# Plain float32 products on two 64-column halves of TensorE in place of split rounded operands, in a two-layer hybrid backbone

## The chip, the cores and the metric

The kernel runs on one core of one Trainium2 chip. The metric is device time in microseconds of one execution. The profile is of one execution, taken by the hardware profiler; the page and the trace rows come from it. Engines are named as the profile names them: PE is TensorE (its weight loads are listed apart, as PEld), DVE is VectorE, ACT is ScalarE, POOL is GpSimd, SP is SyncE, which issues most DMAs here.

## What is computed

1024 latent tokens and 256 context tokens of width 1024 go through two layers and a last RMSNorm. Both layers are `x += gate * mixer(adaLN(RMSNorm(x)))`. Layer 0 is windowed attention with 16 query heads of 64 columns, 4 key heads and a sink logit per head; layer 1 is multi-head latent attention of every latent token over all 1280 tokens. The core of it, cut from the reference:

```
# layer 0: q, k, v, g = split(h @ w_in);  q, k of latent tokens get axial rope
s_loc = einsum("bqhgd,bkhd->bhgqk", q, k) * scale          # own block of 128 and its two neighbours
s_ctx = einsum("bqhgd,bchd->bhgqc", q, kc) * scale         # all 256 context tokens
p = softmax_with_sink(concatenate([s_loc, s_ctx]), sink)
yx = (p @ v * silu(gx)) @ w_out
# layer 1: cq, ckv, kr, g = split(h @ w_in)
q = rms_norm(cq, q_norm) @ w_uq                            # 16 heads of 64 + 32 (rope)
kv = rms_norm(ckv, kv_norm) @ w_ukv                        # 16 heads of 64 + 64
s = (qn . kn + qr . kr) * scale                            # kr is shared by the heads
yx = (softmax(s) @ v * silu(gx)) @ w_out
```

All inputs and outputs are float32.

## The kernel before

**Split operands.** Before, most products are made of three terms. An operand x is kept as two rounded float32 arrays (type `F32R`): `hi`, a rounded copy made by ACT, and `lo`, the rest, `x - hi`, made by DVE or POOL (`split`, L279 to L282). `mm3` (L284 to L288) then issues three matmuls into the same PSUM bank, hi by hi, lo by hi, hi by lo: lines L286, L287 and L288 of the profile. All split operands live in one large SBUF arena `R` of type `F32R` (arena_r), plain float32 data in a second, `F` (arena_f). PSUM is the tile `PB` of eight banks of 512 columns.

**Stages.**

1. The opening: adaLN columns (L840, L850), norm and transposes (L883), and layer 0's values (`v_part`, L912 and L917, which are the same three terms).
2. Layer 0's projections in blocks of 256 columns (`proj_t`), each 128 x 512 piece eight steps of `mm3`, while DVE works through the adaLN vectors of both layers (L508) that are summed over partitions on PE (L519: float32 matmuls with one column of ones, each into its own group of 32 columns of the array).
3. Layer 0's attention, 40 units of one tile of 128 queries and one key head with its four query heads (`UnitA`). `score` makes a head's logits: K stands as hi and lo in the upper and lower 64 rows, so that two matmuls (L698, L699) of 128 rows give a piece, 256 context keys and 256 or 384 window keys. DVE masks and takes the minimum (L705), ACT the exponential (L711), PE turns blocks of 128 keys (L728), the result is split, and `PV` applies it in two terms (L738) to V, whose hi and lo stand side by side in the 128 columns. `outproj` is `mm3` again.
4. Layer 1's projections, among them two rounds of sums that save products (`set_steps`), and the expansion of K and V per head from `ckvT` (`make_K`, `make_V`).
5. Layer 1's attention, 16 units of a pair of heads and 512 queries (`UnitB`). For each block of 128 keys `score` issues five terms, each for the two heads at once in the upper and the lower 64 rows of the array (L1820); ACT makes the exponential (L1830); POOL sums the exponentials of the ten blocks (L1836, DVE in the last unit). `top` (L1786) makes rounded logits of the next unit for its maxima, reduced on DVE (L1792), turned (L1800) and put into q as four extra rows. `PV` (L1843) is plain float32: two heads, each a matmul of 128 rows and 64 columns, in the left and the right half of the array. `fin2` (L1854) sums the denominators over partitions, float32 in two halves too. POOL and DVE prepare the layer's output weights between units (`wo_cut`), part of which takes a trip through DRAM (`wb_d`).
6. The output product in sums that save products (`out_sets`), norm and stores.

**What sets the order.** The opening and stages 2 and 5 are issued in the order of the code. From the last blocks of stage 2 up to the start of stage 5 the instructions are recorded in a `Plan` and issued by a list scheduler (`emit`): each engine takes, of what is ready by the planner's costs, the oldest. The cost of a matmul in it is

```
if eng == "tensor":
    half = 0.5 if aps[1].shape[0] < 128 else 1
    return (0.108 if name == "transpose" else half * (0.0135 + n * 0.000417)), 0.45
```

with n the columns of the result, whatever the type. Engines run their own queues in order; semaphores are set between them.

Of the kernel before, what the change touches and what calls it, by code (L numbers as in the profile page):

```python
# [28 lines left out]
R_KB = 152  # L29
# [188 lines left out]
def kernel(ctx: ExitStack, tc: tile.TileContext, t, out, dbg=None):  # L218
# [7 lines left out]
    R = cpool.tile([128, R_KB * KB], F32R, name="arena_r")  # L226
# [6 lines left out]
    q0_d = dpool.tile([4, 2, 2, 64, NT, 2, 128], F32, name="q0_d")  # L233
    g0_d = dpool.tile([8, 128, TOK], F32, name="g0_d")
    x1_d = dpool.tile([TOK, D], F32, name="x1_d")
    qn_d = dpool.tile([8, 128, 2, SEQ], F32, name="qn_d")
    qr_d = dpool.tile([4, 128, 2, SEQ], F32, name="qr_d")
# [3 lines left out]
    wb_d = dpool.tile([18, 128, 2, 512], F32, name="wb_d")  # L241
# [37 lines left out]
    def split(hi, lo, src, lo_eng=None):  # L279

        nc.scalar.copy(hi, src)  # L281
        (lo_eng or nc.vector).tensor_sub(lo, src, hi.bitcast(F32))  # L282

    def mm3(o, a, b, first, last):  # L284
        (ah, al), (bh, bl) = a, b
        nc.tensor.matmul(o, ah, bh, start=first, stop=False)  # L286
        nc.tensor.matmul(o, al, bh, start=False, stop=False)  # L287
        nc.tensor.matmul(o, ah, bl, start=False, stop=last)  # L288
# [46 lines left out]
    def norm_x(src, xr, junk):  # L335
        x = xr.next()
        load(out=x, in_=src)
        st = sm_ring()
        nc.scalar.activation(junk, x, AF.Square, accum_out=st[:, 0:1])
        nc.gpsimd.tensor_scalar(st[:, 1:2], st[:, 0:1], 1.0 / D, EPS, ALU.mult, ALU.add)  # L340
        nc.gpsimd.tensor_tensor(st[:, 2:3], st[:, 1:2], mhalf, ALU.pow)
        nc.vector.tensor_scalar_mul(x, x, st[:, 2:3])
        return x

    def turn_x(x, xt, j):
        for q in range(2):
            ps = shp(pst(), 4, 128)
            for c in range(4):
                nc.tensor.transpose(ps[:, c, :], x[:, (4 * q + c) * 128 : (4 * q + c + 1) * 128], ident)
            nc.scalar.copy(xt[:, 4 * q : 4 * q + 4, j * 128 : j * 128 + 128], ps)  # L350

    def build_x(p, src, xr, xtr, junk):

        xt = shp(xtr.next(), 8, 256)
        for j in range(2):
            turn_x(norm_x(src(2 * p + j), xr, junk), xt, j)
        return xt

    def build_h(p, xt, hT, A, B, fast=False, ks=range(8)):

        w = 1 if p == 0 else 0
        for k in ks:
            nc.vector.tensor_scalar(xt[:, k, :], xt[:, k, :], A[:, k, w : w + 1], B[:, k, w : w + 1], ALU.mult, ALU.add)
            if k % 2:
                hi = hT[:, 0, k - 1 : k + 1, :]
                nc.scalar.copy(hi, xt[:, k - 1 : k + 1, :])
                eng = nc.vector if fast or k % 4 == 1 else nc.gpsimd
                eng.tensor_sub(hT[:, 1, k - 1 : k + 1, :], xt[:, k - 1 : k + 1, :], hi.bitcast(F32))

# [13 lines left out]

    def load_w(dst, src, stage, nk, n, lo_eng=None, col0=0, k0=0):

        per = max(1, 512 // n)
        for k in range(k0, nk, per):
            st = shp(stage.next(), per, n)
            load(out=st, in_=src[k * 128 : (k + per) * 128, col0 : col0 + n].rearrange("(k p) n -> p k n", p=128))
            split(dst[:, 0, k : k + per, :], dst[:, 1, k : k + per, :], st, lo_eng or nc.gpsimd)  # L390
# [17 lines left out]
    hT = [r_at(16 * p, 2, 8, 256) for p in range(NP)]  # L408
    wst = [80, 96]
    kT = r_at(112, 4, TOK)  # L410
    V = r_at(132, NT, 4, 128)
    cosa = f_at(0, SEQ)
    sina = f_at(10, SEQ)
    stg = Ring(F, [4, 6, 8], 512)
    ev = Ring(F, [38, 40, 42, 44, 46], 512)
    qst = Ring(F, [34, 48], 1024)
# [24 lines left out]
    def fetch(bi, eng=nc.gpsimd):  # L441

        wt[bi] = r_at(wst[bi % 2], 2, 8, 256)
        src = w_in[:, blocks[bi] : blocks[bi] + 256].rearrange("(k p) n -> p k n", p=128)
        got = []

        def get(i):
            got.append(shp(stg.next(), 2, 256))
            load(out=got[i], in_=src[:, 2 * i : 2 * i + 2, :])

        def cut(i):
            ks = slice(2 * i, 2 * i + 2)
            split(wt[bi][:, 0, ks, :], wt[bi][:, 1, ks, :], got[i], eng)

        def second():
            cut(0)
            get(3)
            cut(1)
            cut(2)

        for i in range(3):
            get(i)
        later(1, second)
        later(2, lambda: cut(3))
# [82 lines left out]
    for p in (1, 3):  # L547
        two = R[:, 16 * p * KB : 16 * (p + 2) * KB]
        hw.append(two.rearrange("p (q s k n) -> p q s k n", q=2, s=2, k=8))
    swap = [(i + 16) % 32 for i in range(32)]  # L550

    def proj_t(bi, gp, c):
        W, c0 = wt[bi], blocks[bi]
        ps = PB[:, 4, :] if (bi, gp) == (9, 0) else pss()
        for cc in (c,) if gp else range(2):
            if gp:
                o = shp(ps, 2, 256)
            else:
                o = ps[:, cc * 256 : cc * 256 + 256]
            for k in range(8):  # L560
                if gp:
                    m = [hw[gp][:, :, s, k, :] for s in range(2)]
                else:
                    m = [hT[0][:, s, k, :] for s in range(2)]
                mm3(o, [W[:, s, k, cc * 128 : cc * 128 + 128] for s in range(2)], m, k == 0, k == 7)
# [10 lines left out]
        if gp == 0:  # L576
            if c0 == 1024:
                u = shp(ps, 2, 256)
                for e in range(2):
                    kh = kT[:, e::2, 0:256]  # L580
                    split(kh[0:64], kh[64:128], u[64 * e : 64 * e + 64])
            else:
                q = shp(qst.next(), 2, 2, 2, 128)
                u = shp(ps, 2, 2, 128)
                split(q[:, :, :, 0].bitcast(F32R), q[:, :, :, 1].bitcast(F32R), u)

                def store():
                    for cc in range(2):
                        dst = q0_d[c0 // 256, cc, :, :, 0:2].rearrange("e p t s n -> (e p) (t s n)")
                        load(out=dst, in_=q[:, cc].rearrange("p t s n -> p (t s n)"))  # L590

                later(1, store)
# [9 lines left out]
        def rest():  # L602
            if c0 == 1024:
                q = shp(qst.next(), 2, 512)
                for e in range(2):
                    es = slice(64 * e, 64 * e + 64)
                    nc.vector.tensor_add(q[0:64, e], a[es], r[es])
                khs = [kT[:, 2 * c + e, t0 : t0 + 512] for e in range(2)]
                for e in range(2):
                    nc.scalar.copy(khs[e][0:64], q[0:64, e])  # L610
                for e in range(2):
                    nc.vector.tensor_sub(khs[e][64:128], q[0:64, e], khs[e][0:64].bitcast(F32))
                return
            q = shp(qst.next(), 4, 2, 128)
            split(q[:, :, 0].bitcast(F32R), q[:, :, 1].bitcast(F32R), shp(a, 4, 128))
            dst = q0_d[c0 // 256, c, :, :, t0 // 128 : t0 // 128 + 4].rearrange("e p t s n -> (e p) (t s n)")
            later(1, lambda: load(out=dst, in_=q.rearrange("p t s n -> p (t s n)")))
# [9 lines left out]
    wstg = Ring(F, [4, 6, 12, 34, 36], 512)  # L627
# [1689 lines left out]
```

## Time and profile before

| what | us |
|---|---|
| median of 3 runs | 1476.91 (1476.58 to 1477.49) |
| the profiled execution | 1476.32 |
| its span, first to last instruction | 1474.5 |
| PE busy | 1453.1 (99%), 8988 records |
| DVE, ACT, POOL busy | 1129.9, 747.3, 872.8 |
| layer 0's attention, about 304 to 674 us | 370 |
| layer 1's attention, about 914 to 1397 us | 483 |

A row of a group reads: line, engine, operation, output <- inputs, rows * columns of the array, input shape, count, then busy time, mean duration in ns, and idle time before it with what ended it. A row of the timeline reads: start in us, length of the row, engine, line, operation, count. Durations of matmuls overlap their successors', because they are pipelined; the distance between starts is what a matmul costs. A plain float32 matmul that is not a transpose appears as two records of the trace, so 8510 matmuls of the program are 8988 records.

### The profile page before, as it was taken

The numbers are of one execution on the slowest core, as the hardware profiler recorded it, in microseconds if no ns is written. First come the engines' busy times: TensorE is split into PE (matmuls) and PEld (weight loads), VectorE is DVE, ScalarE is ACT, GpSimd is POOL, SyncE is SP. The second block draws the span as 40 slices with busy tenths as digits, with TensorE's granted clock in tenths as the row PEclk, the third lists the DMA queues.
The fourth block names the chain that finished last, engine by engine and source line by source line (L and its number), as shares of the span: only waits on it lengthen the run. The fifth ranks groups of instructions, "written<-read, shape, count | busy, mean of one in ns | idle before, by whom it ended". The sixth has DMA issues, their size and how long they took to land. (4 is left out here: it accounts for less than half of the span.)

```text
span 1474.5 us, 25163 instructions
## 1 busy us (share of the span) xinstructions
PE 1453.1 (99%) x8988; PEld 1179.2 (80%) x8988; DVE 1129.9 (77%) x2065; ACT 747.3 (51%) x1421; POOL 872.8 (59%) x765
## 2 busy tenths in 40 slices
PE   7999999999999999999999999999999999999998
PEld 4888888888888888889888888776777766776586
DVE  4787789738878888878988777677788787676887
ACT  4421222259887888878554522444444443444433
POOL 2463366256464444446400050599999999999886
PEclk9999999999999999999999999999999999999999
DMA  9545645583343332328443566112222232356352
GB/s 336 175 165 179 214 144 178 173 257 112 115 137 120 106 111 93 95 88 257 116 120 104 182 208 204 47 44 65 81 71 69 83 115 83 104 178 209 143 179 100
DMA packets 152214, 204.90 MB, mean 139 GB/s; under 512 B 13452, under 2 KB 101132, under 8 KB 152088
## 3 DMA queue, kind: packets, MB, share of 16 engines
q1 hardware_dynamic: 147112, 196.63, 41.6%
q10 hardware_dynamic: 4976, 6.66, 1.3%
q8 instruction: 71, 1.16, 0.3%
q14 instruction: 55, 0.45, 0.1%
HBM read 143.46 MB, written 55.59 MB: 135 GB/s over the span
## 5 line engine op out<-in xcount | busy, mean ns | idle before, releaser
L286 PE MATMUL PB<-arena_r 128*128 128x512 f32 (+2 forms) x1180 | 432.6, 367 | 1.1 <-DVE arena_f L1262 1.1
L287 PE MATMUL PB<-arena_r 128*128 128x512 f32 (+2 forms) x1180 | 426.9, 362 | 0.5 <-DVE arena_r L282 0.4
L288 PE MATMUL PB<-arena_r 128*128 128x512 f32 (+2 forms) x1180 | 426.5, 362 | 0.0
L1836 POOL TENSOR_TENSOR arena_f<-arena_f 128x1024 f32<-128x1024 f32 x120 | 293.0, 2441 | 9.4
L286 PEld LDWEIGHTS PB<-arena_r 128*128 128x128 f32 x1180 | 222.5, 189 | 46.0 <-issue 10.6
L288 PEld LDWEIGHTS PB<-arena_r 128*128 128x128 f32 x1180 | 222.5, 189 | 33.3
L287 PEld LDWEIGHTS PB<-arena_r 128*128 128x128 f32 x1180 | 222.6, 189 | 32.4 <-DVE arena_r L282 0.8
L1820 PE MATMUL PB<-arena_r 64*128 64x512 f32 (+1 forms) x1600 | 229.3, 394 | 0.0
L1830 ACT ACTIVATE arena_f<-PB 128x1024 f32<-128x1024 f32 x160 | 164.6, 1028 | 119.0 <-PE PB L1820 90.4
L1792 DVE TENSOR_REDUCE krF<-PB 128x1 f32<-128x512 f32 (+1 forms) x264 | 166.9, 677 | 54.5 <-PE PB L1786 54.5
L1820 PEld LDWEIGHTS PB<-arena_r 64*128 64x128 f32 (+1 forms) x1600 | 179.9, 185 | 13.7 <-issue 5.2
L705 DVE CUSTOM_DVE_ANT_0 arena_f<-PB,arena_f,small 128x256 f32<-128x256 f32 (+1 forms) x288 | 148.2, 525 | 50.6 <-PE PB L699 32.4
L281 ACT CAST arena_r<-PB 128x512 fp32r<-128x512 f32 (+2 forms) x207 | 115.3, 563 | 106.5 <-PE PB L288 68.3
L282 DVE TENSOR_TENSOR arena_r<-PB,arena_r 128x512 fp32r<-128x512 f32 (+2 forms) x207 | 134.3, 661 | 25.9 <-ACT arena_r L281 25.1
L281 ACT CAST arena_r<-arena_f 128x512 fp32r<-128x512 f32 (+1 forms) x156 | 90.7, 613 | 124.6 <-PE PB L288 33.7
L1843 PE MATMUL PB<-arena_f 128*64 128x512 f32 x640 | 145.9, 595 | 0.0
L282 POOL TENSOR_TENSOR arena_r<-arena_f,arena_r 128x512 fp32r<-128x512 f32 (+1 forms) x48 | 67.6, 1428 | 104.7 <-ACT arena_r L281 82.6
L711 ACT ACTIVATE arena_f<-arena_f,small 128x640 f32<-128x640 f32 (+2 forms) x160 | 119.1, 744 | 15.5 <-DVE small L705 13.9
L508 DVE SCALAR_TENSOR_TENSOR arena_f<-arena_f,small 128x512 f32<-128x512 f32 x98 | 114.1, 1209 | 11.3 <-DMA arena_f<-ada_w 11.1
L738 PE MATMUL PB<-arena_r 128*128 128x512 f32 x336 | 118.8, 429 | 0.1
L1786 PE MATMUL PB<-arena_r 64*128 64x512 f32 (+1 forms) x768 | 113.9, 355 | 0.1
L728 PE MATMUL PB<-ident,arena_f 128*128 128x128 f32 x672 | 108.7, 272 | 0.1
(251 smaller groups left out, 2237.3 us busy)
## 6 DMA issues: line engine op xcount, KB each, us to landing
arena_f<-ada_w SPq DMA_DIRECT2D x96, 256.0 KB, 4.0
arena_r<-q_d SPq DMA_DIRECT2D x160, 128.0 KB, 2.8
arena_f<-a_w_in SPq DMA_DIRECT2D x40, 256.0 KB, 3.5
arena_f<-x_d SPq DMA_DIRECT2D x18, 512.0 KB, 5.5
arena_f<-b_w_in SPq DMA_DIRECT2D x36, 256.0 KB, 3.1
wb_d<-arena_r SPq DMA_DIRECT2D x18, 512.0 KB, 3.0
arena_r<-wb_d SPq DMA_DIRECT2D x18, 512.0 KB, 6.8
arena_f<-x SPq DMA_DIRECT2D x16, 512.0 KB, 5.3
```

The source lines that it names most:

```text
L281: nc.scalar.copy(hi, src)
L282: (lo_eng or nc.vector).tensor_sub(lo, src, hi.bitcast(F32))
L286: nc.tensor.matmul(o, ah, bh, start=first, stop=False)
L287: nc.tensor.matmul(o, al, bh, start=False, stop=False)
L288: nc.tensor.matmul(o, ah, bl, start=False, stop=last)
L705: nc.vector.tensor_tensor_reduce(o, S, mk, -A_SCALE, prev, ALU.add, ALU.min, mx)
L711: nc.scalar.activation(P, P, AF.Exp, bias=nm, scale=-1.0, accum_out=self.den[:, h : h + 1])
L1792: nc.vector.reduce_max(self.mxp[:, e, b : b + 1, i], bank[:, 0:n], AX.X)
L1820: nc.tensor.matmul(PB[:, b + e, :], k[r, s, cs], q[r, sq], start=i == 0, stop=i == 4)
L1830: nc.scalar.activation(E, PB[:, b : b + 2, :], AF.Exp)
L1836: eng.tensor_add(acc, acc, E)
L1843: nc.tensor.matmul(PB[r, 7, :], Vq[:, c, h, :], E[:, e], start=c == 0, stop=c == NT - 1)
```

## The change

Every product but `top` is plain float32. `mm3` gives way to `mm`: two matmuls, one for each half of 64 columns of the stationary operand, into the upper and the lower 64 partitions of the result. No operand is split; all `split` and cut steps go, copies that remain are single. The arena `R` becomes float32 and smaller, a small arena `TT` of type `F32R` (arena_t) holds the rounded K and q that `top` needs, and the addresses of nearly everything change. In `UnitA`, `score` takes 64 rows and two halves of columns (quarter tiles of 64 x 64), and `PV` one half, left and right in turn over the blocks. In `UnitB`, `score` has two terms instead of five, each on four quarter tiles; the blocks from number 6 on are added to the denominators on PE (`self.db`), in place of sums on POOL; q is loaded twice, once for each arena. Output weights stay in SBUF, without the trip through `wb_d`. The planner's costs are the same. The program's matmuls go from 8510 to 6890. Neighbouring matmuls of different tile size (the array addressed as 128x128, 128x64, 64x128, 64x64 or 128x32) go from 83 to 1155.

```diff
-    def mm3(o, a, b, first, last):
-        (ah, al), (bh, bl) = a, b
-        nc.tensor.matmul(o, ah, bh, start=first, stop=False)
-        nc.tensor.matmul(o, al, bh, start=False, stop=False)
-        nc.tensor.matmul(o, ah, bl, start=False, stop=last)
+    HALF = [slice(64 * e, 64 * e + 64) for e in range(2)]
+
+    def mm(o, a, b, first, last):
+        for r in HALF:
+            nc.tensor.matmul(o[r], a[:, r], b, start=first, stop=last)
...
     def v_part(p, b):
         h, W = hT[p], wt[0]
         for k in (2 * b, 2 * b + 1):
             for j in range(2):
-                js = slice(j * 128, j * 128 + 128)
                 o = PB[:, p, j * 256 : j * 256 + 256]
-                for s in range(2):
-                    nc.tensor.matmul(o, h[:, 0, k, js], W[:, s, k, :], start=k == j == s == 0, stop=False)
...
+                for r in HALF:
+                    w = slice(j * 128 + r.start, j * 128 + r.stop)
+                    nc.tensor.matmul(o[r], h[:, k, w], W[:, k, :], start=k == j == 0, stop=j == 1 and k == 7)
...
         def score(self, h, later=False):
...
+            r = HALF[h % 2]
+            q = qT[r, h // 2]
...
-                nc.tensor.matmul(S, q[:, 0], kT[:, g, ko : ko + n], start=True, stop=False)
-                nc.tensor.matmul(S, q[:, 1], kT[:, g, ko : ko + n], start=False, stop=True)
+                for w in HALF:
+                    nc.tensor.matmul(S[w], q[:, w], kT[r, g, ko : ko + n], start=True, stop=True)
...
-            PT = shp(ptr.next(), 2, 512)
-            split(shp(PT[:, 0], 4, 128), shp(PT[:, 1], 4, 128), pt)
+            PT = ptr.next()
+            nc.scalar.copy(shp(PT, 4, 128), pt)
...
-            for s in range(2):
-                nc.tensor.matmul(
-                    self.pv, V[:, self.chunks[ci], self.g, :], PT[:, s],
-                    start=ci == 0 and s == 0, stop=ci == self.m - 1 and s == 1,
-                )
+            nc.tensor.matmul(
+                self.pv[HALF[ci % 2]], V[:, self.chunks[ci], self.g, :], PT, start=ci < 2, stop=ci > self.m - 3
+            )
...
-    CUT = 3
+    CUT = 1
+    ND = 6
...
         def prep(self):
-            q = self.q.bitcast(F32)
-            load(out=q[:, 0:2], in_=qn_d[self.pair, :, :, self.ts])
...
+            for q in (self.qh.bitcast(F32), self.q):
+                load(out=q[:, 0], in_=qn_d[self.pair, :, self.ts])
+                for e in range(2):
+                    r = 32 * ((2 * self.pair + e) % 4)
+                    load(out=q[64 * e : 64 * e + 32, 1], in_=qr_d[self.pair // 2, r : r + 32, self.ts])
...
-            terms = ((kt, 0, 0, 64), (kt, 0, 1, 64), (kt, 1, 0, 64), (KR, 0, 2, 64), (KR, 1, 3, 36))
+            terms = ((self.kt, 64), (KR, 36))
             for i in range(i0, i1):
-                k, s, sq, n = terms[i]
-                for e in range(2):
-                    r = slice(64 * e, 64 * e + n)
-                    nc.tensor.matmul(PB[:, b + e, :], k[r, s, cs], q[r, sq], start=i == 0, stop=i == 4)
+                k, n = terms[i]
+                for w in HALF:
+                    ks = slice(c * 128 + w.start, c * 128 + w.stop)
+                    for e in range(2):
+                        r = slice(64 * e, 64 * e + n)
+                        nc.tensor.matmul(PB[w, b + e, :], k[r, ks], self.q[r, i], start=i == 0, stop=i == 1)
...
             if c == 1:
                 eng.tensor_add(acc, self.E[0], E)
-            elif c:
+            elif 1 < c < ND:
                 eng.tensor_add(acc, acc, E)
...
                     nc.tensor.matmul(PB[r, 7, :], Vq[:, c, h, :], E[:, e], start=c == 0, stop=c == NT - 1)
+                if c >= ND:
+                    for e, r in enumerate(HALF):
+                        nc.tensor.matmul(self.db[r, :], ones, E[:, e], start=c == ND, stop=False)
```

Lines of the profile before and their counterparts after: L286 to L288 become L284; L912 and L917, L802; L698 and L699, L616; L728, L645; L738, L654; L1820, L1581; L1786, L1547; L1800, L1561; L1843, L1604; L1854, L1618; new is L1607.

More of the change, by code (lines that the diff above doesn't have):

```diff
@@ L225 @@
     PB = ppool.tile([128, 8, 512], F32, name="PB")
-    R = cpool.tile([128, R_KB * KB], F32R, name="arena_r")
+    R = cpool.tile([128, R_KB * KB], F32, name="arena_r")
+    TT = cpool.tile([128, T_KB * KB], F32R, name="arena_t")
     F = cpool.tile([128, F_KB * KB], F32, name="arena_f")
@@ L382 @@
     sm_ring8 = SmallRing(6, 8)
[L384 to L390, printed above, removed]
     def rope(o, u, cos, sin, nh, dim, tmp):
@@ L439, in next_item, with fetch @@
             fn()
-    def fetch(bi, eng=nc.gpsimd):
-        wt[bi] = r_at(wst[bi % 2], 2, 8, 256)
+    def fetch(bi):
+        wt[bi] = r_at(wst[bi % 2], 8, 256)
         src = w_in[:, blocks[bi] : blocks[bi] + 256].rearrange("(k p) n -> p k n", p=128)
-        got = []
         def get(i):
[L448 to L464, printed above, removed]
+            load(out=wt[bi][:, 2 * i : 2 * i + 2, :], in_=src[:, 2 * i : 2 * i + 2, :])
+        get(0)
+        get(1)
+        later(1, lambda: (get(2), get(3)))
     ada0 = AdaLN(0)
@@ L1552 @@
     h1_two(two)
-    h1_two_out(two)
     x1_square(6)
@@ L1568 @@
         kv_mm(ti)
-        now, two = two, turn_two()
-        h1_two_out(now)
+        two = turn_two()
         if ti < 3:
@@ L1615 @@
     for n, i in enumerate((2, 3, 4, 5, 0, 1)):
-        ps = product(a12r[i], B21)
-        x = outs.next()
+        ps = product(a12[i], B21)
+        x = home(i, 0, 0)
         nc.vector.tensor_add(x, ps, p1s[i])
@@ L1665, in uk_cut @@
         for k in range(2):
[L1666 to L1670 removed]
+            load(out=dst[:, k], in_=t["b_w_ukv"][k * 128 : k * 128 + 128, c0 : c0 + 1024])
     for i in range(8):
```

690 lines of the change are left out of this document (206 added, 484 removed).

## The prediction

> **What bounds the kernel now.** I read the page's busy line first, then the waits of TensorE alone, then stage windows, then the timeline for the distance from one matmul's start to the next.
>
> ```profile
> span 1474.5 us, 25163 instructions
> PE 1453.1 (99%) x8988; PEld 1179.2 (80%) x8988; DVE 1129.9 (77%) x2065; ACT 747.3 (51%) x1421; POOL 872.8 (59%) x765
> ```
> ```profile
> PE PB L840 <- DMA arena_f<-ada_w: 8.5, 3, 7.6
> PE PB L1275 <- DVE arena_r L282: 1.2, 1, 1.2
> ```
> A busy PE need not be full, but here it is: it waits 8.5 us for the first `ada_w` pieces, and every other wait on its list is 1.2 us or less. So all time after the opening is matmuls standing nose to tail, and what the change does to the *start-to-start distance* of matmuls is what it does to the time. Everything taken off DVE, ACT and POOL (the splits) is worth nothing in the sum, because PE hides it already.
>
> The windows of the first layer's attention and of the second layer's attention, columns PE, PEld, DVE, ACT, POOL, say the same by stage (behind them the granted clock, 1.00):
>
> ```profile
> 304.00:674.00 370.00, 369.51 (x2274) 323.90 (x2273) 289.09 (x868) 302.19 (x729) 183.34 (x325) 1.00 0.40 124
> 914.00:1397.00 483.00, 482.59 (x3499) 352.71 (x3500) 361.23 (x464) 215.75 (x256) 431.93 (x218) 1.00 0.31 100
> ```
> POOL's 432 of 483 us is the nearest second, and the change gives it less work (no cuts, five sums of nine).
>
> **The price of a product, before and after.** In the timeline, rounded-float matmuls of the three-term product:
>
> ```profile
> 902.15 0.39 PE L286 MATMUL PB<-arena_r 128*128 128x512 f32 x1
> ...
> 902.83 0.39 PE L286 MATMUL PB<-arena_r 128*128 128x512 f32 x1
> ...
> 911.09 0.28 PE L286 MATMUL PB<-arena_r 128*128 128x256 f32 x1
> ...
> 911.45 0.28 PE L286 MATMUL PB<-arena_r 128*128 128x256 f32 x1
> ```
> The duration column (0.39) overlaps; the starts tell: three terms take 0.68 us at 512 columns (0.227 each), 0.36 at 256. What the change puts there already stands in the trace: L1843 (probabilities times values) is plain float32 on two 64-column halves.
>
> ```profile
> 999.57 2.74 PE L1843 MATMUL PB<-arena_f 128*64 128x512 f32 x12
> 1002.15 0.39 PE L1800 MATMUL PB<-ident,krF 128*64 128x128 f32 x4
> 1002.36 4.46 PE L1843 MATMUL PB<-arena_f 128*64 128x512 f32 x20
> 1006.76 0.50 PE L286 MATMUL PB<-arena_r 128*128 128x512 f32 x1
> 1007.09 0.40 PE L287 MATMUL PB<-arena_r 128*128 128x512 f32 x1
> ```
> L1843 has 320 instructions in the program and 640 records: a float32 matmul is two records. From 999.57 to 1002.15 run 12 records, three pairs of halves: **0.86 us a pair**, against 0.68 for three rounded terms. The two halves run at the same time, each with two records of 0.43, so a half alone takes the same 0.86. The loads of the halves' weights are in that price already. At other widths I scale: 0.43 at 256, 0.48 at 288, 0.645 at 384 (estimates).
>
> The same rows price a **switch of tile size**. Five pairs from 1002.36 end at 1006.66; L286 on the full array starts at 1006.76 (0.10 lost), and its successor comes 0.33 later instead of 0.23 (0.10 more, its weights were not loaded ahead). Into a 64-column size:
>
> ```profile
> 996.37 0.64 PE L1820 MATMUL PB<-arena_r 64*128 64x512 f32 x4
> 996.95 1.08 PE L1843 MATMUL PB<-arena_f 128*64 128x512 f32 x4
> 997.85 1.03 PE L1854 MATMUL PB<-arena_f,small 128*64 128x512 f32 x4
> ```
> 996.37 to 996.95 is two steps of 0.23 and 0.12 over; the pair then takes 0.90 instead of 0.86. I take 0.15 us into a 64-column size, 0.20 into a 128-column one. Before has 83 such switches in its program, after 1,155.
>
> **The change, term by term** (counts from these groups, shapes kept apart):
>
> ```profile
> L286 PE MATMUL PB<-arena_r 128*128 128x512 f32 x852 | 337.3, 396 | 0.0
> L286 PE MATMUL PB<-arena_r 128*128 128x256 f32 x248 | 71.0, 286 | 0.0
> L286 PE MATMUL PB<-arena_r 128*128 128x288 f32 x80 | 24.4, 305 | 1.1 <-DVE arena_f L1262 1.1
> L912 PE MATMUL PB<-arena_r 128*128 128x256 f32 x160 | 23.7, 291 | 0.2
> L738 PE MATMUL PB<-arena_r 128*128 128x512 f32 x336 | 118.8, 429 | 0.1
> L698 PE MATMUL PB<-arena_r 128*128 128x256 f32 x192 | 55.3, 296 | 0.3
> L698 PE MATMUL PB<-arena_r 128*128 128x384 f32 x96 | 33.5, 349 | 0.0
> ```
> (a) Products: 852 x (0.86 - 0.68) = 153; 248 x (0.43 - 0.36) = 17; 80 x (0.48 - 0.40) = 6; the opening's values (160 L912 and, by the code, half as many L917 at 0.12, then 80 pairs at 0.43) 6. **+182.**
>
> (b) to (d) First layer's attention. Its rows in the timeline:
>
> ```profile
> 501.29 0.60 PE L728 MATMUL PB<-ident,arena_f 128*128 128x128 f32 x4
> 501.65 0.71 PE L738 MATMUL PB<-arena_r 128*128 128x512 f32 x2
> 502.19 0.28 PE L698 MATMUL PB<-arena_r 128*128 128x256 f32 x1
> 502.31 0.28 PE L699 MATMUL PB<-arena_r 128*128 128x256 f32 x1
> 502.43 0.34 PE L698 MATMUL PB<-arena_r 128*128 128x384 f32 x1
> 502.61 0.34 PE L699 MATMUL PB<-arena_r 128*128 128x384 f32 x1
> 502.79 0.60 PE L728 MATMUL PB<-ident,arena_f 128*128 128x128 f32 x4
> ```
> (b) A head's score pieces take 0.24 and 0.36; after, a pair of quarter tiles (64 rows, 64 columns) each takes 0.43 and 0.645: 192 x 0.19 + 96 x 0.285 = +64. Two heads use different rows and may overlap: fully overlapped the 144 us of scores would halve (-8 in all). Parts of neighbouring heads mostly have another tile size between them, so I take **+60**.
>
> (c) The values: two terms of 0.227 become one half alone, 0.86. Of the 168, a pair of halves stands together only about eleven times, so 157 x 0.86 - 336 x 0.227 = **+59**.
>
> (d) The planner still prices any matmul at 0.0135 + 512 x 0.000417 = 0.227 us and spreads halves singly. PE in the middle of the first attention; L728/L645 turn probabilities, L738/L654 apply them to values, L698-L699/L616 are scores, L286-L288/L284 the output product. Before:
>
> ```order
> L728 MATMUL PB<-ident,arena_f 128x128 x4
> L738 MATMUL PB<-arena_r 128x512 x2
> L698 MATMUL PB<-arena_r 128x256
> L699 MATMUL PB<-arena_r 128x256
> L698 MATMUL PB<-arena_r 128x384
> L699 MATMUL PB<-arena_r 128x384
> ```
> PE after, at a like place:
>
> ```order
> L654 MATMUL PB<-arena_r 64x512
> L645 MATMUL PB<-ident,arena_f 128x128 x3
> L616 MATMUL PB<-arena_r 64x256 x2
> L284 MATMUL PB<-arena_r 64x512
> L616 MATMUL PB<-arena_r 64x384
> L645 MATMUL PB<-ident,arena_f 128x128
> L616 MATMUL PB<-arena_r 64x384
> L284 MATMUL PB<-arena_r 64x512 x2
> ```
> Nearly every row is now a switch of size, and a lone L284 or L616 leaves half the array empty. 124 runs of L284 have an odd count; each wastes half a pair: 124 x 0.43 = **+53**.
>
> (e), (f) Second layer's attention.
>
> ```profile
> 1011.68 1.38 PE L1820 MATMUL PB<-arena_r 64*128 64x512 f32 x10
> 1012.84 0.68 PE L1786 MATMUL PB<-arena_r 64*128 64x512 f32 x4
> ```
> A block of keys costs 1.16 us (five terms, two row halves at once). After: two terms, each on four quarter tiles. On PE around a unit's end, before (L1820 scores, L1786 maxima, L1843 values, L1854 denominators, L1800 the turned maxima):
>
> ```order
> L1820 MATMUL PB<-arena_r 128x512 x10
> L1786 MATMUL PB<-arena_r 128x256 x8
> L1820 MATMUL PB<-arena_r 128x512 x4
> L1843 MATMUL PB<-arena_f 64x512 x2
> L1854 MATMUL PB<-arena_f,small 64x512 x2
> ```
> and after (L1581, L1547, L1604, L1607 and L1618, L1561):
>
> ```order
> L1581 MATMUL PB<-arena_r 64x512 x8
> L1547 MATMUL PB<-arena_t 128x256 x8
> L1581 MATMUL PB<-arena_r 64x512 x4
> L1604 MATMUL PB<-arena_f 64x512 x10
> L1561 MATMUL PB<-ident,krF 64x128 x2
> L1604 MATMUL PB<-arena_f 64x512 x4
> L1607 MATMUL PB<-arena_f,small 64x512 x2
> ```
> Eight quarter-tile matmuls replace ten, the maxima stay as they were but need a switch in and out, and L1607 is new. Before shows no quarter tile. The bounds: four at once, 0.86 a term; two at once, 1.72. Nearest row for four at once:
>
> ```profile
> 123.93 1.04 PE L519 MATMUL PB<-arena_f,small 128*1 128x512 f32 x8
> ```
> These are four float32 matmuls, each in its own column group: eight records end within 1.04 us, two rounds of 0.43 and a tail; two at a time would need four rounds. So 0.86 a term: 160 x (1.72 - 1.16) = **+90**. New L1607: 16 units x 4 blocks x 0.86 = **+55**. Values, maxima and L1618 keep their count and price.
>
> (g) Switches: 752 into 64 columns or fewer x 0.15 + 403 into 128 x 0.20 - 83 x 0.18 = **+179**. 334 of them go between 128x64 and 64x64 tiles, which before does not show: 0 to 0.15 each, 0 to 50 us in all; I take 0.15, as in the nearest rows. The Trainium skill, page "TensorEngine Tiling", Key Properties, says that a change of tiling mode, not only of the tile, drains TensorE; it speaks against this layout, by it the sum stands at +678, and were these 334 free it would be +628. The two switches in the rows above, 0.10 and more lost at each, agree.
>
> At nothing: splits, cuts, the trip of `wb_d` through DRAM, the second load of q, the copy of K into two arenas. PE's own work covers them; with that cover gone they would still be less than what went. No stall of size goes, so nothing is late next.
>
> Sum: 182 + 60 + 59 + 53 + 90 + 55 + 179 = +678. The profiled execution took 1476.3 us (span 1474.5), the median is 1476.9; 1476.3 + 678 = 2154, say **2150 us**. The first attention goes from 370 to about 680, the second from 483 to about 690.
>
> **Rivals.**
> *Two quarter tiles at a time.* If matmuls start strictly in program order, a tile's second record holds back the next tile's first, and a score term takes 1.72: 160 x 2 x 0.86 = +275, end about 2430. The Trainium skill's page "TensorE: Matmul & The Clock Gate", Part 3, states strict order of starts. Against it: the L519 row, though its weights are one column wide. 0.10.
> *Switches cost little* between sizes that the change uses: 2154 - 179 = 1975. Against: every switch in the trace paid. 0.05.
> *PE starves in the first attention,* its order having been planned with matmuls nearly four times too cheap:
>
> ```profile
> L711 ACT ACTIVATE arena_f<-arena_f,small 128x640 f32<-128x640 f32 (+2 forms) x160 | 119.1, 744 | 15.5 <-DVE small L705 13.9
> ```
> One exponential (744 ns) bare at each of 160 heads is +119, end 2270. Against: a slower PE gives the others more time. 0.06.
> *Not slower: float32 from the arena streams at the rounded rate,* 0.227 a record instead of 0.43. The float32 work of (a) to (f) after is about 1,570 us; 47% less is -740, end 1415. It decides below 0.49 us a pair. L1843 and L1854, same shape and type, stand at 0.86. 0.03, of which 0.01 within 0.2% (3 us, about what can be told here).
>
> **Numbers.** The sum 0.76. Its own bounds: heads overlapping and free switches between half and quarter tiles, 2154 - 68 - 50 = 2036; 0.20 at every switch and half the starvation, 2154 + 38 + 60 = 2250. Widened by some 2% for the scaled widths: 2010 to 2290. Faster 0.02, same 0.01, slower 0.97.
>
> **Right or wrong.** The profile after should show PE 98% or more busy and its waits still short; L284 pairs 0.86 apart; eight L1581 in 1.72; 0.1 to 0.2 between rows of different tile size; every other engine's share lower. Eight L1581 in 3.4, L284 pairs under 0.6, or waits of PE over 50 us would refute a step.

## The result: 1.43 times the time before, and the profile after

| | before | after |
|---|---|---|
| median, us | 1476.74 (4 runs, 1476.57 to 1477.49) | 2116.68 (4 runs, 2116.35 to 2117.21) |
| the profile's span, us | 1474.5 | 2115.0 |
| matmul records | 8988 | 12040 |
| layer 0's attention, us | 370 | 650 |
| layer 1's attention, us | 483 | 692 |

After takes 1.433 times the time of before (95% interval 1.4308 to 1.4357). Forecast were 2150 us, with a range of 2010 to 2290, and 680 and 690 us for the two attentions.

The busy line of the page after, and the list of what TensorE waits for:

```profile
span 2115.0 us, 29890 instructions
PE 2092.6 (99%) x12040; PEld 767.0 (36%) x12040; DVE 798.6 (38%) x1674; ACT 622.4 (29%) x1191; POOL 512.2 (24%) x500
```
```profile
PE PB L739 <- DMA arena_f<-ada_w: 8.3, 3, 7.9
PE PB L782 <- DVE arena_f L775: 2.2, 2, 1.4
PE PB L616 <- DVE small L622: 2.1, 5, 0.5
PE PB L1300 <- ACT arena_r L1306: 1.4, 2, 0.8
```
As before, the only wait of size is for the first weights; the one wait that the new order of layer 0's attention brings (L616 behind DVE) is 2.1 us in all. DVE lost 331 us of work and POOL 361, and none of it shows in the time: TensorE still works without gaps, with more to do. The windows of the two attentions (columns PE, PEld, DVE, ACT, POOL, then the clock):

```profile
378.00:1028.00 650.00, 647.39 (x3000) 223.81 (x2998) 188.42 (x688) 290.68 (x710) 114.25 (x221) 1.00 0.14 45
1320.00:2012.00 692.00, 692.00 (x4878) 247.00 (x4877) 311.19 (x470) 203.99 (x233) 248.80 (x132) 1.00 0.13 41
```
TensorE is busy for all but 2.6 us of the first and for all of the second, and the next engine for less than half of either, so TensorE is the bound in both; the granted clock is 1.00, as before.

**What a product costs.** The timeline around the end of a unit of layer 1's attention, with values (L1604) and the new denominators (L1607) in turn:

```profile
1499.84 1.03 PE L1607 MATMUL PB<-arena_f,small 128*64 128x512 f32 x4
1500.70 1.03 PE L1604 MATMUL PB<-arena_f 128*64 128x512 f32 x4
1501.56 1.03 PE L1607 MATMUL PB<-arena_f,small 128*64 128x512 f32 x4
```
A pair of halves is 0.86 us from start to start, no matter which line it comes from, since the tile size stays. In the scores of the same attention:

```profile
1481.71 0.73 PE L1547 MATMUL PB<-arena_t 64*128 64x512 f32 x4
1482.37 1.95 PE L1581 MATMUL PB<-arena_r 36*64 36x512 f32 x16
1484.25 0.73 PE L1547 MATMUL PB<-arena_t 64*128 64x512 f32 x4
```
Sixteen records are eight quarter-tile matmuls, two terms. They take 1.88 us with a switch: four quarter tiles stand at once, 0.86 a term and 0.15 for the switch. L1547 has two steps of a rounded matmul, 0.45, and takes 0.66, so its switch costs 0.2. Blocks are now 2.54 us apart where the maxima stand between them.

The rows of layer 0's attention (L616 scores, L645 transposes, L654 values, L284 output product):

```profile
501.17 1.07 PE L654 MATMUL PB<-arena_r 128*64 128x512 f32 x2
502.17 0.55 PE L645 MATMUL PB<-ident,arena_f 128*128 128x128 f32 x3
502.65 1.29 PE L616 MATMUL PB<-arena_r 64*64 64x256 f32 x8
503.87 1.07 PE L284 MATMUL PB<-arena_r 128*64 128x512 f32 x2
504.88 0.33 PE L645 MATMUL PB<-ident,arena_f 128*128 128x128 f32 x1
```
A lone half of L654 or L284 (two records) holds the array for 1.00 us, 0.86 and a switch of 0.14, as long as a pair would. One transpose, 0.11 where another follows it, takes 0.25 with its switch (504.88 to 505.13, where the next row starts). That is how this stage grew by 280 us.

**Where the time went,** from the trace: the distance from each matmul's start to the next one's, summed by line. Before and after: output products and projections (L286 to L288, now L284) 715.8 and 946.9; layer 0's scores 84.6 and 173.7, its values 90.2 and 150.7, its transposes 55.9 and 103.6; layer 1's scores (L1820, L1581) 190.4 and 301.8, the maxima 77.4 and 105.1; the denominators L1607 none and 54.9. These come to 622 of the 640 us that all lines of PE gained. The part of the span in which TensorE is not busy went from 21 to 22 us, so it explains none of it.

### The profile page after: what moved, and what is told of

Read it like the earlier page. It is cut to its first block, busy times and chain, and to the rows that moved or that the text cites. A ratio compares the mean times of both kernels' runs of the same rounds, so it can differ in the third digit from the quotient of the medians.

```text
span 2115.0 us, 29890 instructions
## 1 busy us (share of the span) xinstructions
PE 2092.6 (99%) x12040; PEld 767.0 (36%) x12040; DVE 798.6 (38%) x1674; ACT 622.4 (29%) x1191; POOL 512.2 (24%) x500
## 4 chain that ended last, share of the span: by engine, by line
PE 98%; DMA 1%; DVE 0%; issue 0%; ACT 0%; POOL 0%; POOLq 0%
PE PB L284 45%; PE PB L1581 14%; PE PB L616 8%; PE PB L1604 7%; PE PB L654 7%; PE PB L1547 5%; PE PB L645 5%; PE PB L1607 3%; PE PB L802 2%; DMA arena_f<-ada_w 1%; PE PB L672 1%; PE PB L1618 1%; PE PB L782 1%; PE PB L739 0%; PE PB L1300 0%
## 5 line engine op out<-in xcount | busy, mean ns | idle before, releaser
L284 PE MATMUL PB<-arena_r 128*64 128x512 f32 (+2 forms) x4272 | 882.8, 533 | 0.0
L284 PEld LDWEIGHTS PB<-arena_r 128*64 128x64 f32 x4272 | 306.2, 137 | 474.8 <-issue 412.2
L1581 PE MATMUL PB<-arena_r 36*64 36x512 f32 (+1 forms) x2560 | 313.5, 602 | 0.0
L616 PE MATMUL PB<-arena_r 64*64 64x256 f32 (+1 forms) x1152 | 189.2, 433 | 2.4 <-DVE small L622 2.1
L647 ACT COPY arena_r<-PB 128x512 f32<-128x512 f32 x168 | 94.0, 585 | 328.4 <-PE PB L645 327.3
L654 PE MATMUL PB<-arena_r 128*64 128x512 f32 x336 | 166.5, 610 | 0.0
L1604 PE MATMUL PB<-arena_f 128*64 128x512 f32 x640 | 151.8, 595 | 0.0
L1597 POOL TENSOR_TENSOR arena_f<-arena_f 128x1024 f32<-128x1024 f32 x60 | 141.1, 2351 | 12.8 <-ACT arena_f L1591 12.5
L1581 PEld LDWEIGHTS PB<-arena_r 36*64 36x64 f32 (+1 forms) x2560 | 81.8, 132 | 141.2 <-issue 136.7
L1595 POOL TENSOR_TENSOR arena_f<-arena_f 128x1024 f32<-128x1024 f32 x15 | 35.3, 2353 | 396.8 <-ACT arena_f L1591 396.8
L645 PEld LDWEIGHTS PB<-ident,arena_f 128*128 128x128 f32 x672 | 72.9, 140 | 121.6 <-issue 93.9
L1547 PE MATMUL PB<-arena_t 64*128 64x512 f32 (+1 forms) x768 | 115.9, 396 | 0.0
L645 PE MATMUL PB<-ident,arena_f 128*128 128x128 f32 x672 | 114.8, 287 | 0.2
L616 PEld LDWEIGHTS PB<-arena_r 64*64 64x64 f32 x1152 | 57.5, 131 | 122.0 <-DVE small L622 59.9
L1547 PEld LDWEIGHTS PB<-arena_t 64*128 64x128 f32 x768 | 56.0, 185 | 124.4 <-DVE krF L1553 91.7
L284 PE MATMUL PB<-arena_r,arena_f 128*64 128x512 f32 x448 | 99.2, 594 | 0.0
```

Source lines behind the costliest of these rows:

```text
L284: nc.tensor.matmul(o[r], a[:, r], b, start=first, stop=last)
L616: nc.tensor.matmul(S[w], q[:, w], kT[r, g, ko : ko + n], start=True, stop=True)
L645: nc.tensor.transpose(pt[:, h, :], self.Ps[h][:, ci * 128 : ci * 128 + 128], ident)
L654: nc.tensor.matmul(self.pv[HALF[ci % 2]], V[:, self.chunks[ci], self.g, :], PT, start=ci < 2, stop=ci > self.m - 3)
L1547: nc.tensor.matmul(bank[:, o : o + n], self.qh[r, s, bs], k[r, n0 : n0 + n], start=s == 0, stop=s == 1)
L1581: nc.tensor.matmul(PB[w, b + e, :], k[r, ks], self.q[r, i], start=i == 0, stop=i == 1)
```

## The experiments

Unless said otherwise each is the changed kernel with one edit, 2116.68 us unedited. Experiments 5 and 8 have ten and four runs, each of the others one. The 13 runs of the kernel before that go with experiments 5 to 8 lie within 2.7 us (0.2%), so a few us between single runs say nothing.

**1. Full array.** What does a float32 product cost on 128 columns in one instruction, without halves?

```diff
 def mm(o, a, b, first, last):
-    for r in HALF:
-        nc.tensor.matmul(o[r], a[:, r], b, start=first, stop=last)
+    nc.tensor.matmul(o, a, b, start=first, stop=last)
```


> The changed kernel with every product of mm issued as one float32 matmul on all 128 columns instead of two on 64. Theory A (a float32 matmul costs two records of 0.43 us at 512 columns, however many columns of the array it uses): L284 still costs 0.86 a product, and what goes is the lone halves (124 x 0.43 = 53) and 159 switches of tile size (996 instead of 1155, about 0.15 each, 24): 2116 - 77, about 2040 us. Theory B (the halves are what brings the price down to 0.86; on the full array a record streams half as fast): products at 1.72, 852 x 0.86 + 248 x 0.43 + 80 x 0.48 = 878 more, less those 77: about 2920 us.

2075.11 us. Its timeline in layer 0's attention:

```profile
505.59 1.98 PE L283 MATMUL PB<-arena_r 128*128 128x512 f32 x4
507.41 0.82 PE L644 MATMUL PB<-ident,arena_f 128*128 128x128 f32 x6
```
Four records are two matmuls on the full array, 1.82 us with the switch into them: 0.86 each, exactly what a pair of halves costs. So the price is that of plain float32, two records of 0.43, and neither of the halves nor of the layout; the halves bring nothing here. What they cost is 42 us, in lone halves and in switches around them (L284's distances 946.9, this line's 898.5; the values, still lone halves, went from 150.7 to 159.8: no half of a product is left for them to stand beside). Theory A's 2040 is missed by 35 us. Some 13 of them are halves of products and values that had stood side by side already, as shown below under (b) to (d), and TensorE is idle 7 us longer (30 for 22); the rest is open.

**2. Scores of layer 1 on row halves** of 64 x 128, the size that the maxima have, in place of quarter tiles.

```diff
-                for w in HALF:
-                    ks = slice(c * 128 + w.start, c * 128 + w.stop)
-                    for e in range(2):
-                        r = slice(64 * e, 64 * e + n)
-                        nc.tensor.matmul(PB[w, b + e, :], k[r, ks], self.q[r, i], start=i == 0, stop=i == 1)
+                ks = slice(c * 128, c * 128 + 128)
+                for e in range(2):
+                    r = slice(64 * e, 64 * e + n)
+                    nc.tensor.matmul(PB[:, b + e, :], k[r, ks], self.q[r, i], start=i == 0, stop=i == 1)
```


> The changed kernel with the second attention's scores on two row halves (64 rows, 128 columns) instead of four quarter tiles, two float32 matmuls a term. Theory A (price by records, not by width): still 0.86 a term, and the maxima have the same tile size, so 300 switches go (0.13 into quarter tiles, 0.20 into the maxima's tile, 150 each, about 50): 2116 - 50, about 2066 us. Theory B (float32 on 128 columns streams half as fast): 1.72 a term, 160 x 2 x 0.86 = 275 more, less 50: about 2340 us.

2062.03 us, 54.7 less, with 300 switches fewer: 0.18 each. The timeline of this kernel, at the place shown above:

```profile
1461.27 1.88 PE L1580 MATMUL PB<-arena_r 36*128 36x512 f32 x8
1462.59 1.03 PE L1547 MATMUL PB<-arena_t 64*128 64x512 f32 x4
1463.46 1.88 PE L1580 MATMUL PB<-arena_r 36*128 36x512 f32 x8
```
Blocks are 2.19 us apart, before 2.54: 0.35 for two switches. With no switch left a block is just two score terms of 0.86 and the 0.45 of the maxima: four matmuls now do what eight quarter tiles did, in the same two steps of 0.86, so two row halves stand at once as four quarter tiles do.

**3. Pairs.** The planner takes the two halves of a product, and the two quarter tiles of a score piece in layer 0's attention, as one operation, so that nothing comes between them.

```diff
-        for r in HALF:
+        for j, r in enumerate(HALF):
+            plan.join = j
             nc.tensor.matmul(o[r], a[:, r], b, start=first, stop=last)
+        plan.join = 0
```


> The changed kernel with the planner told to issue the two halves of a product, and the two column halves of a score piece in the first attention, as one: same matmuls, other order. Theory A (a lone half leaves half the array empty and costs 0.43 us, a switch about 0.15): 124 x 0.43 = 53 less, 102 fewer switches 15 less: about 2048 us. Rival (lone halves overlap with their neighbours, the order costs nothing): 2116 within 5. Second rival (the fine order hid waits of TensorE that now show): above 2116, with more than 20 us of waits of TensorE.

2040.36 us, 76 less. The distances of L284 fell from 946.9 to 902.7, of L616 from 173.7 to 148.8, of L654 by 6. In its timeline the products stand in whole pairs, while each lone half of the values (L664) still takes a full 1.0 us:

```profile
499.62 1.94 PE L291 MATMUL PB<-arena_r 128*64 128x512 f32 x8
501.49 0.86 PE L625 MATMUL PB<-arena_r 64*64 64x384 f32 x4
502.28 1.07 PE L664 MATMUL PB<-arena_r 128*64 128x512 f32 x2
503.29 0.65 PE L625 MATMUL PB<-arena_r 64*64 64x256 f32 x4
```
There are 1053 switches of size instead of 1155; 102 of 0.15 are 15 us of the 76. The other 61 are put down to halves and score pieces that had stood alone.

**4. All denominators on POOL** again, as before the change.

```diff
-    ND = 6
+    ND = NT
...
-                nc.tensor.matmul(self.db[r, :], ones, acc[:, e], start=False, stop=True)
+                nc.tensor.matmul(self.db[r, :], ones, acc[:, e], start=True, stop=True)
```


> The changed kernel with the denominators of all ten blocks summed on POOL again, no L1607. Theory A (TensorE bounds, POOL has room): 64 pairs x 0.86 = 55 less, about 2062 us. Rival (the last sums come late and hold the denominators' matmul, one sum of 2.35 us bare in each of 15 units, 35): about 2097 us, with waits of TensorE for POOL of that size.

2070.16 us, 46.5 less: 54.9 of L1607 went, and one wait came, in the second of the 16 units:

```profile
PE PB L1618 <- POOL arena_f L1597: 5.1, 1, 5.1
```
So at this length of a unit, which holds 43 us of TensorE, POOL could have kept the sums. Moving them to TensorE cost what the forecast said and gave only those 5 us back.

**5. Before without its low parts.** The kernel before, with the low parts of most products not made (134 instructions of DVE and 110 of POOL fewer) and the high part put in all three terms. It leaves the low terms out of what is computed.

```diff
     def mm3(o, a, b, first, last):
         (ah, al), (bh, bl) = a, b
+        al, bl = ah, bh
```


> The kernel before, with the low parts of most three-term products left out of the making (weights, layer 1's inputs, output operands: 134 DVE and 110 POOL instructions less), and the high part used in their place in all three matmuls. It leaves the low terms out of the result; TensorE's matmuls are the same in number, size and shape. Theory A (TensorE bounds from end to end, the splits are hidden): 1476, no more than 10 us less. Rival (the splits held TensorE, and their going is a gain that the change has too): 30 us or more less, below 1446.

1476.71 us against 1477.16 of before in the same rounds, ratio 0.9998 (0.9988 to 1.0007). The page's busy line:

```profile
PE 1454.7 (99%) x8988; PEld 1177.8 (80%) x8988; DVE 1014.5 (69%) x1931; ACT 749.0 (51%) x1421; POOL 739.1 (50%) x655
```
DVE lost 115 us and POOL 134, and the time stayed. These splits were paid on engines that had room, and a change that removes them has nothing to win from them. The splits of layer 0's queries, keys and probabilities and of layer 1's keys are still made here; for them the same is argued, from the short waits of TensorE, and not shown.

**6. Values of layer 0 two blocks at a time,** left and right half together.

```diff
-            u.PV(ci)
+            if ci % 2:
+                u.PV(ci - 1)
+                plan.join = 1
+                u.PV(ci)
+                plan.join = 0
+            elif ci == u.m - 1:
+                u.PV(ci)
```


> The changed kernel with the values of the first attention applied two blocks at a time, left and right half together: 72 pairs and 24 lone halves in place of 157 runs. Theory A: 61 x 0.86 = 52 less, 37 fewer switches 6 less: about 2058 us. Rival (lone halves were covered by neighbours): 2116 within 10.

2082.78 us, 33.9 less, not 58. The values themselves went from 150.7 to 118.2; two things stood against the rest. Theory A charges each of the 157 runs with 0.86 us, but some 15 halves of the values had shared the array with a half of L284 (below, under (b) to (d)), and their 13 us could not be won again. And the products had 148 runs of an odd number of halves, where they had 124, which at 0.43 each is 10 us:

```profile
502.05 1.07 PE L290 MATMUL PB<-arena_r 128*64 128x512 f32 x2
503.06 0.66 PE L651 MATMUL PB<-ident,arena_f 128*128 128x128 f32 x4
```
One half of L290 alone, 1.01 us. The groups of products of 512 columns, of the changed kernel and of this one:

```profile
L284 PE MATMUL PB<-arena_r 128*64 128x512 f32 x2960 | 731.0, 597 | 0.0
```
```profile
L290 PE MATMUL PB<-arena_r 128*64 128x512 f32 x2960 | 742.5, 597 | 0.0
```
The products are busy 11.5 us longer, so part of what the values gain is paid there. The two together, an estimate, account for most of the 24 us that are missing.

**7. Pairs, and the planner told the price:** 0.00084 us a column for float32.

```diff
+            if name != "transpose" and aps[1].dtype == F32:
+                return 0.002 + n * 0.00084, 0.45
```


> Halves planned as one, and the planner given the measured price of plain float32 (0.00084 us a column for a half, 0.86 for a pair at 512) instead of 0.227 a matmul. Theory A (the order is a matter of switches and lone halves, not of the price in the plan): as with halves planned as one alone, 2040, less 54 fewer switches x 0.15 = 8: about 2032 us. Rival (TensorE's order was planned badly because matmuls were priced too low): 2000 or less.

2047.11 us, no better than pairs alone (2040.36) and 15 above theory A's 2032. There are 54 switches fewer, but by the distances from start to start the products take 20 us more than in pairs (922.7), the scores 6.5 more and the values 14 less; why this order is no better is open. A half of the values that stands alone was still priced at 0.43, half of what it takes. Its largest wait is the one of the opening, which is issued in the order of the code, here put down to ACT in place of the weights' DMA:

```profile
PE PB L751 <- ACT PB L775: 8.2, 1, 8.2
```
The next is 2.2 us. Beyond the halves set apart, the wrong price in the planner cost nothing that the right one brings back: TensorE was not short of work in either.

**8. The best plain layout,** experiments 1, 2, 4 and 6 together and layer 0's scores on 64 rows by 128 columns: 573 switches.

```diff
+        nc.tensor.matmul(o, a, b, start=first, stop=last)
...
+                nc.tensor.matmul(S, q, kT[r, g, ko : ko + n], start=True, stop=True)
...
+    ND = NT
```


> Plain float32 as in the change, but on all 128 columns wherever the operand has them (products, scores of both attentions on row halves), values two blocks at a time, denominators on POOL. Switches 573 instead of 1155. Theory A (the gains add): full array 42, scores on rows 55, denominators 47 (each as measured), values 58, lone halves of the first attention's scores 25, 86 more switches 13: 240 less, about 1877 us, still far above 1476. Rival (TensorE now waits for others, POOL's sums above all): 1930 or more, with over 50 us of waits of TensorE.

1917.58 us (1915.79 to 1918.4), 1.298 times before (1.2959 to 1.3002): 199 us less than the changed kernel, 40 over what theory A expected and still below the rival's 1930. Its busy line, the first rows of its waits and the source view of the last sums say where:

```profile
PE 1856.3 (97%) x7568; PEld 915.0 (48%) x7568; DVE 819.1 (43%) x1678; ACT 621.3 (32%) x1191; POOL 653.7 (34%) x560
```
```profile
PE PB L1627 <- POOL arena_f L1606: 26.2, 11, 7.0
PE PB L743 <- DMA arena_f<-ada_w: 8.6, 2, 7.8
PE PB L620 <- DVE small L626: 5.9, 13, 0.5
PE PB L1310 <- ACT arena_f L1008: 4.0, 1, 4.0
```
```profile
  POOL arena_f L1606: 62.9, 25
```
The part of the span in which TensorE is not busy is 60 us here, 22 in the changed kernel. Experiments 1 and 4, whose gains were taken as measured, had 7 and 5 us of this already, so idle time accounts for some 25 of the 40 us; the rest is open. POOL's sums, which held TensorE for 5 us in experiment 4, hold it in 11 of the 16 units now that a unit is shorter. The list of waits has 26.2 us for it, the source view 62.9. The source view adds up what the matmuls (PE, 26.2) and their weight loads (PEld, 36.7) stood idle for the same sums. The next two tell what the wait is worth.

**9 and 10. The same with four, or two, blocks' denominators on TensorE** (POOL keeps the other sums).

```diff
-    ND = NT
+    ND = 8
```


> This is plain_best with the last six blocks' denominators back on TensorE, as in the changed kernel. Theory A (TensorE is the bound, and what waited on GpSimd's sums in plain_best, 62.9 us behind POOL L1606, goes when the sums are shorter): 1917.6 - 63 + 55 = about 1910, with no wait left on POOL. Rival (the waits on POOL stay, only the products come back): 1917.6 + 55 = about 1973.

> This is plain_best with only the last two blocks' denominators on TensorE: 16 units x 2 pairs x 0.86 = 27.5 us of products come back. Theory A (GpSimd's sums then end before the denominators are wanted): 1917.6 - 63 + 27.5 = about 1882. Rival (the waits on POOL stay): about 1945.

`ND = 6`, as in the changed kernel, puts four blocks there (the expectation says six, but its 55 us are those of four) and gave 1938.91 us; `ND = 8` two blocks and 1913.86 us. The waits after `ND = 8`:

```profile
PE PB L743 <- DMA arena_f<-ada_w: 7.7, 1, 7.7
PE PB L620 <- DVE small L626: 5.9, 13, 0.5
...
PE PB L1627 <- POOL arena_f L1606: 0.7, 1, 0.7
```
The wait on POOL is gone, as theory A said, and yet the time fell by 3.7 us, which is no clear difference for a single run on another chip, where it said 36. What failed is the 63 us that the expectation took from the source view as time to be won. By the distances from start to start, the values that stand ahead of those sums (L1613) went from 166.3 to 138.3 us, and the new denominators took 28.3: some 28 us had been waited, near the 26.2 of the list of waits, and the same came back as products. `ND = 6` agrees: 55 of products less 28 are 27, and 21 were measured. So the wait is worth what the list of PE's own waits says. All three stay over 430 us above the kernel before.

**11. One more switch in and out** ahead of each of layer 1's 160 blocks: a transpose of the identity, whose result the scores overwrite. 1458 switches, 303 more.

```diff
+                if i == 0:
+                    nc.tensor.transpose(PB[:, b, 0:128], ident, ident)
                 for w in HALF:
```


> This is the changed kernel with one more 128x128 transpose of the identity ahead of each of the second attention's 160 blocks, its result overwritten: 303 more switches of tile size. Theory A (a switch costs the drain of about 0.10 and the exposed weights of 0.05 to 0.06 behind it): 160 x (0.109 + 0.154 + 0.147) = +66, about 2182. Rival 1 (only the drain): +49, about 2166. Rival 2 (switches are free, and the time after is all products): +17, about 2134.

2179.98 us, 63.3 more. Of these 160 x 0.109 = 17 are the transposes; 46 for 303 switches are 0.15 each (17 of the 160 places had a switch there already). Its timeline:

```profile
1541.42 1.09 PE L1583 MATMUL PB<-arena_r 36*64 36x512 f32 x8
1542.44 0.33 PE L1578 MATMUL PB<-ident 128*128 128x128 f32 x1
1542.69 1.09 PE L1583 MATMUL PB<-arena_r 64*64 64x512 f32 x8
```
0.25 for the transpose, 0.11 and a switch of 0.14; the score term ahead of it takes 1.02, 0.86 and 0.16. So the price of a switch holds where switches are put in on purpose too. The drain alone (2166) and free switches (2134) are refuted.

## Why the prediction was right, point by point

**The bound.** The step "all time after the opening is matmuls standing nose to tail" held on both sides. Experiment 5 shows what it implies: the splits that it leaves out were free, so their going put nothing on the change's credit side.

**(a) Products.** 0.86 a pair against 0.68 for three rounded terms was read from L1843 and holds for L284, whose pairs are 0.86, and at other widths by the scaling (in experiment 1 two records are 0.43 at 256 columns and 0.49 at 288). Experiment 1 shows that it is the price of the type: 0.86 with one matmul on all 128 columns too. The rival by which the product would go at 0.227 a record is refuted by the same rows. The Trainium skill's page "FP8 and Floating Point Precision", TensorE Precision Notes, says that true float32 is four passes through the array; the trace agrees in size, 0.86 against 0.227 for one rounded matmul, 3.8 times, though it shows two records. Three rounded terms are cheaper than one plain product by that ratio.

**(b), (c) and (d), layer 0's attention.** The mechanism was right: quarter tiles and lone halves keep the array as long as whole ones. Some 25 us are left of the sum's error of 38 after (g). That is a remainder, not a measurement, but the stage points here: 650 us, where 680 were forecast. What the terms overlooked is that lone halves of two lines can meet. Of the lone halves, 29 stretches of L284 and 34 of L654 in the trace are of one record, that is, a half of one line beside a half of the other:

```profile
516.03 0.64 PE L284 MATMUL PB<-arena_r 128*64 128x512 f32 x1
516.03 0.64 PE L654 MATMUL PB<-arena_r 128*64 128x512 f32 x1
516.51 0.59 PE L284 MATMUL PB<-arena_r 128*64 128x512 f32 x1
516.51 0.59 PE L654 MATMUL PB<-arena_r 128*64 128x512 f32 x1
517.04 0.65 PE L616 MATMUL PB<-arena_r 64*64 64x256 f32 x4
```
The two start together, and the next tile size starts 1.01 us later, where (c) charges 0.86 for the one and (a) and (d) together 0.86 for the other. Some 15 such meetings (an estimate, from half of 29 and half of 34), each worth 0.86, are 13 of the 25 us. Experiment 3, which sets the halves of a product together, took 44 us off L284, switches included; (d) had 53. The scores, without the switches into their 225 stretches (0.147 each), take 141 us, which is (b)'s 144 less the 4 that it took off for overlap of two heads: that term was right. The remaining 12 us are not assigned.

**(e) Layer 1's scores.** Four quarter tiles at once, 0.86 a term, from the L519 row of one-column weights, carried over to quarter tiles of 64 columns: 1.88 us for 16 records with the switch. The rival of two at a time would show 3.4 and is refuted: the second record of one quarter tile does not hold back the first of the next. In the trace the first records of the four tiles of a term start about 7 ns apart, and the four second records follow 0.43 to 0.48 us later in the same order. The Trainium skill's page "TensorE: Matmul & The Clock Gate", Part 3, states that matmuls start and end strictly in program order; the trace agrees, and what fails is the rival's step from that order to a wait between tiles.

**(f)** 55, measured 54.9; experiment 4 gave 46.5 of it back and 5 us of a wait.

**(g) Switches.** The step that was mis-sized. The sizes measured in the changed kernel: 0.15 us into a tile of 64 columns or fewer (0.58 for a lone score piece of 256 columns, 0.43 of it work, with half tiles on both sides as with transposes on both), 0.15 into a 128 x 128 transpose where 0.20 was taken, 0.20 into L1547. So 752 x 0.147 + 249 x 0.154 + 154 x 0.204 - 15 = 165, not 179. The 0.20 came from L286 behind L1843, a rounded matmul; the transposes, most of the switches into 128 columns, are cheaper. The 334 between half and quarter tiles, which had no row before, cost what the others do. Experiments 2 and 11 put 0.18 and 0.15 on a switch, one by taking 300 away and one by adding 303. The rival of cheap switches is refuted. That a change of size drains TensorE is what the Trainium skill's page "TensorEngine Tiling", Key Properties, states, and the trace agrees: the second record of a lone half takes 0.52 us to the next start where it takes 0.43 within a stretch, so the switch holds back the next matmul by 0.09; the first record behind a switch takes 0.48, which is the other 0.05.

**Starvation.** The waits of TensorE are 15 us in all, most of it the opening; the rival asked for 119. Its premise, an order planned with matmuls nearly four times too cheap, is true of the planner, but the engines that feed a slower TensorE had the more time, as the forecast argued. Experiment 7 gave the planner the price and won nothing.

The sum: 678 were forecast and 640 measured. Of the 38 between them, 14 are (g), some 13 the meetings of lone halves, and the rest is not assigned.

## What to carry to other kernels

Price a change of number format by the distance from start to start of matmuls that already stand in the trace in that format, and look for idle time on the engine that bounds before crediting what other engines save. A layout of part tiles costs twice: a lone half takes as long as a whole, and every change of tile size about 0.15 us. Take what a wait costs TensorE from the list of PE's own waits: the view by source line adds the idle time of the weight loads to that of the matmuls, and here it showed 62.9 us for a wait worth 26 to 28.

## What the runs showed of the hardware

A plain float32 matmul takes two records of 0.43 us at 512 columns, on 64 or on 128 columns of weights alike (experiment 1), and four quarter tiles take no longer than two row halves (experiment 2). The halves' weights load in that time. A switch of tile size costs 0.15 us: 0.09 ahead of it, by which the next matmul starts later (0.52 for 0.43), and 0.05 in the first record behind it (0.48 for 0.43). Where a rounded 64 x 128 matmul follows it costs about 0.20.
